# Turning both heads' probabilities with one DMA transposition per query block

## The chip, the cores and the metric

One NeuronCore of one Trainium2 chip runs the whole program. The metric is the device time of one execution in microseconds (us); the figure for the kernel before is the median of three runs. Of one execution there is a profile with a trace: TensorE (PE, with its weight loads as PEld), VectorE (DVE), ScalarE (ACT), GpSimd (POOL), and the sync engine SP, which issues the DMAs.

## The reference

One decoder layer over 16 meta tokens and 512 real positions, model width 1024. From one projection of the normalized input come two attention branches of 16 heads each: MLA (low-rank queries and keys with a rotary part) and FoX (forget gates, added to the scores as differences of a running sum). Both use the same causal attention:

```python
s = jnp.einsum('bhqd,bhkd->bhqk', qb, k, preferred_element_type=jnp.float32) * scale
if cq is not None:
    s = s + (cq[..., :, None] - cum[:, :, None, :])
s = jnp.where(key_pos[None, :] <= qpos[:, None], s, -jnp.inf)
p = jax.nn.softmax(s, axis=-1)
return jnp.einsum('bhqk,bhkd->bhqd', p.astype(v.dtype), v)
```

Each branch's result is gated, multiplied by its own output matrix and by a sigmoid gate; the sum goes through one more matrix, is normalized and added to the input.

## The kernel before

The program has three parts: a prologue (normalization, small projections, the first queries and keys), the attention part (its last `ov` matmul starts at 409.6 us) and the merge with the two branch matrices and the output matrix. Products in full precision are made of three half products: operands are split into a high part (ScalarE) and a low remainder (VectorE or GpSimd), and `passes` and `unit` multiply high by high, low by high and high by low.

The attention part has 16 stages, two heads each: for pair 0 to 7 first the FoX stage, then the MLA stage. I number them 0 to 15, so even stages are FoX and odd ones MLA. In a stage:

- `scores(0)` and `scores(1)` multiply queries and keys of query blocks 0 to 2 and of block 3 (128 queries each, groups `GRP`), VectorE adds the mask and finds the row bound, ScalarE takes the exponential into `sf`.
- `norm(0)` and `norm(1)` divide by the row sums and write the probabilities as 16-bit high and low parts into `pn[0]` (blocks 0 to 2) and `pn[1]` (block 3). ScalarE writes the high parts (L824), VectorE the low ones (L825), GpSimd those of the meta tokens (L811 to L816). Query block b has 2b + 3 tiles of 128 x 128 for each head: one for the meta tokens, and a high and a low one for each key block. That is 3, 5, 7 and 9.
- Then DMA transpositions on SP's queue turn them, one for each block and head, into `pts[0]` and `pts[1]` (keys on partitions, 9 tiles by 512 queries). `pn` and `pts` exist once, and every stage uses them again.
- `values()` multiplies the turned probabilities (`pt`) by the values (`vp`, turned by a DMA transposition as well) into `ov`. It runs after the next stage's `scores(0)`, and its first matmuls read the meta tile of all four query blocks, so it needs the whole set of transpositions.

TensorE's order is the order in which the program is written (`manual_schedule`): between the pieces of a stage stand the projections of the next one (`fq`, `fk`, `mq`, `mk`, `v`, `z`) as filling work. The other engines and SP's queue are ordered by a scheduler, except in a stretch with `keep_in_program_order`. SP takes its instructions one after the other; its queue also holds the weight loads (`wraw`) and the loads of `CT` (forget sums) and `QP` (rotary queries). The DMAs signal through eight semaphores in turn. All issues come from the helper at L91, all matmuls from L97.

`pts` also lends its room, before the first stage, to the rotary queries of the first eight heads (`room`).

Of the kernel before, what the change touches and what calls it, by code (L numbers as in the profile page):

```python
# [11 lines left out]
F32 = mybir.dt.float32  # L12
F32R = mybir.dt.float32r
F16 = mybir.dt.float16
# [9 lines left out]
S = 512  # L24
# [20 lines left out]
PN_STEP = 5  # L45
# [9 lines left out]
def block_kernel(ctx: ExitStack, tc: tile.TileContext, x, meta_tokens, pre_norm_g, w_in, fox_forget_b,  # L55
                 mla_q_norm_g, mla_kv_norm_g, w_uq, w_ukv, w_br_mla, w_br_fox, w_out, post_norm_g,
                 rope_tok, rope_pe, out):
    nc = tc.nc
# [27 lines left out]
    behind, through, first_t, exps, halved, lowered = [], [], [], [], {}, {}  # L86

    def dma(out, src, start=None):

        with tc.issue_after(sums_out[1]) if written[0] and len(sums_out) == 2 else nullcontext():  # L90
            ins = (start or nc.sync.dma_start)(out=out, in_=src)  # L91
        if written[0]:
            tc.keep_in_program_order(ins)
        return ins.ins
# [7 lines left out]
    def split_lo(eng, lo, src, hi):  # L102
        return eng.tensor_tensor(out=lo, in0=src, in1=f32(hi), op=ALU.subtract)  # L103
# [33 lines left out]
    def weights(srcs, wrap):  # L137

        st = {}

        def load():
            if "l" not in st:
                st["l"] = wload(srcs())

        def get():
            load()
            return wrap(wsplit(st["l"]))
        get.load = load
        return get
# [25 lines left out]
    def unit(name, getw, act, nk, sls, done):  # L175

        st = {}
        out = []

        def prep():  # L180
            if "w" not in st:
                st["w"] = getw()
            return True
        for i, sl in enumerate(sls):
            n = sl.stop - sl.start
            for k in range(nk):
                def fn(i=i, sl=sl, k=k, n=n):
                    if "b" not in st:
                        st["b"] = prep()
                        for load in getattr(out[0][1], "nxt", ()):  # L190
                            load()
                    if k == 0:
                        st["ps"] = acc(f"{name}{i}")
                    ps = st["ps"][:, :n]
                    (wh, wl), (ah, al) = st["w"], act(k)
                    for q, (w, a) in enumerate(((wh, ah), (wh, al), (wl, ah))):
                        mm(ps, w(k), a[:, sl], start=(k == 0 and q == 0), stop=(k == nk - 1 and q == 2))
                    if k == nk - 1:
                        done(i, ps)
                out.append((3 * n / 2.4, fn))  # L200
        out[0][1].prep = prep
        if hasattr(getw, "load"):
            out[0][1].load = getw.load
        return out
# [353 lines left out]
    with ExitStack() as att:  # L558

        att.enter_context(tc.manual_schedule(engines={mybir.EngineType.PE}))  # L560
        ac = att.enter_context(tc.tile_pool(name="ac", bufs=1))
# [8 lines left out]
                                channel_multiplier=1, compare_op=ALU.is_ge, fill=NEG)  # L570


        pn = [ac.tile([128, 2, n, 128], F16, tag=f"pn{g}", name=f"pn{g}") for g, n in enumerate((17, 9))]

        pts = [ac.tile([128, 9, 512], F16, tag=f"pt{h}", name=f"pt{h}") for h in range(2)]

        vh = ac.tile([128, 9, 128], F16, tag="vh", name="vh")
        vps = [ac.tile([128, 9, 128], F16, tag=f"vp{s}", name=f"vp{s}") for s in range(2)]
        nc.gpsimd.memset(vh[:, 0], 0.0)
        for b in range(4):  # L580
            nc.gpsimd.memset(pn[b // 3][:, :, PN_STEP * b % 15, :], 0.0)
        gT = []

        wuqh = wuq.rearrange("p k (h e) -> p k h e", e=NOPE + ROPE)
# [36 lines left out]
        def pe_unit(g):  # L621

            def room():
                if g == 0:
                    return [p.rearrange("p a b -> p (a b)")[:, 0 : 8 * S].bitcast(F32).rearrange("p (c s) -> p c s", c=4)
                            for p in pts]
                return gT[0][:, 4:8], gT[1][:, 4:8]

            def results(x):
                if g == 0:  # L630
                    return gT[x][:, 4:6]
                return room()[x][:, 2:4]
            if g == 0:
                nc.sync.dma_start(room()[0][:, 0:2], rope_pe)
            out = []
            w = {}

            def half(xi, ws=None):
                if ws:
                    w[0] = ws  # L640
                return (lambda k: w[0][2 * xi + k][0]), (lambda k: w[0][2 * xi + k][1])

            def srcs():
                if g:

                    tc.keep_in_program_order(nc.sync.dma_start(room()[0][:, 0:2], rope_pe))
                return [wuqh[:, k, 8 * g : 8 * g + 8, NOPE + 16 * x : NOPE + 16 * x + 16]
                        for x in range(2) for k in range(2)]

            for xi in range(2):  # L650
                get = (lambda: half(1)) if xi else weights(srcs, lambda ws: half(0, ws))

                def done(i, ps, xi=xi):
                    r0, tt = room()
                    for cs in range(2):
                        nc.vector.tensor_tensor(out=tt[:, 2 * xi + cs], in0=ps, in1=r0[:, cs], op=ALU.mult)
                out += unit(f"ppe{g}{xi}", get, cq_act, 2, REAL, done)

            def rest(x):

                tt, rr = room()[1], results(x)
                nc.gpsimd.tensor_tensor(out=tt[:, x], in0=tt[:, x], in1=tt[:, 3 - x], op=(ALU.subtract, ALU.add)[x])
                hi, lo = rr[:, 0], rr[:, 1]
                nc.gpsimd.tensor_copy(hi.bitcast(F32R), tt[:, x])
                split_lo(nc.gpsimd, lo.bitcast(F32R), tt[:, x], hi)
                if g:
                    store(x, 0, 8)
                else:

                    for h in range(2):  # L670
                        for i in range(2):
                            r = 64 * h + 32 * i + 16 * x
                            dma(f32(QP[r : r + 16]), rr[16 * h : 16 * h + 16, i])

            def store(x, a, b):
                for i in range(2):
                    dma(qpe_dram[8 * g + a : 8 * g + b, i, x], results(x)[16 * a : 16 * b, i])
            return out, rest, store
# [66 lines left out]
        def attention(br, pr):  # L745
# [55 lines left out]
            def norm(g):  # L801
                def fn():
                    b0, nb_ = GRP[g][0], len(GRP[g])
                    su, ri = (sums[t][:, :, b0 : b0 + nb_] for t in ("su", "ri"))
                    nc.vector.tensor_scalar(out=su, in0=su, scalar1=1.0 / PSCALE, scalar2=None, op0=ALU.mult)
                    nc.vector.reciprocal(ri, su)

                    mt = aw.tile([128, 2, nb_, META], F32, tag=f"mt{g}", name=f"mt{nm_}{g}", bufs=1)
                    src = sfs[g][:, :, 0 : SF_STEP * nb_].rearrange("p h (b c) -> p h b c", b=nb_)[:, :, :, 0:META]
                    dst = pn[g][:, :, 0 : PN_STEP * nb_].rearrange("p h (b t) c -> p h b t c", b=nb_)[:, :, :, 0]  # L810
                    nc.gpsimd.tensor_tensor(out=mt, in0=src, in1=ri.unsqueeze(3).broadcast_to([128, 2, nb_, META]),  # L811
                                            op=ALU.mult)
                    hi, lo, hi2 = (dst[:, :, :, 32 * i : 32 * i + META] for i in range(3))
                    nc.gpsimd.tensor_copy(hi, mt)
                    nc.gpsimd.tensor_tensor(out=lo, in0=mt, in1=hi, op=ALU.subtract)
                    nc.gpsimd.tensor_copy(hi2, mt)  # L816
                    for b in GRP[g]:
                        for h in range(2):
                            sf = sf_of(h, b)[:, META:].rearrange("p (j c) -> p j c", c=128)
                            t0 = PN_STEP * (b % 3) + 1  # L820
                            hi, lo = (pn[g][:, h, t0 : t0 + 2 * b + 2].rearrange("p (j l) c -> p j l c", l=2)[:, :, i]
                                      for i in range(2))
                            rib = sums["ri"][:, h, b : b + 1]
                            nc.scalar.activation(hi, sf, AF.Copy, scale=rib)  # L824
                            nc.vector.scalar_tensor_tensor(out=lo, in0=sf, scalar=rib, in1=hi, op0=ALU.mult,  # L825
                                                           op1=ALU.subtract)
                    for b in GRP[g]:
                        for h in range(2):
                            t0 = PN_STEP * (b % 3)
                            through[:] = [dma(pts[h][:, 0 : 2 * b + 3, 128 * b : 128 * b + 128],  # L830
                                              pn[g][:, h, t0 : t0 + 2 * b + 3].rearrange("p t c -> p (t c)"),
                                              nc.sync.dma_start_transpose)]
                return fn

            def values():
# [37 lines left out]
        g = gate_unit()  # L873
# [3 lines left out]
        for si, (br, pr) in enumerate(stages):  # L877
# [10 lines left out]
            else:  # L888
                g = gate_unit()
# [308 lines left out]
```

## Time and profile before

| what | value |
|---|---|
| runs | 603.93 us median (603.8 to 607.29) |
| profiled execution | 605.73 us, its span 603.9 us |
| granted TensorE clock | 0.998 |
| DMA packets | 219,961, 93.25 MB, mean 154 GB/s |
| of them under 512 bytes | 133,421 |
| share of the 16 DMA engines' span, SP's queue | 66.4% |

Columns of the quoted views: in the waits, the waiting engine with its group, the releaser, then total us, number of waits and the longest. In a timeline, start and length in us, the engine with its line, then the operation with what it writes and reads, and in brackets the idle time ahead of it. A group of SP's issues shows shortest, median and longest in ns. The span is the time from the first to the last instruction of the program.

### The profile page before, as it was taken

The page shows a single profiled execution, that of the slowest core. Times are in us where ns is not written, and L with a number is a line of the kernel's source. Part 1 is how long each engine was busy: PE and PEld are TensorE (multiplying, and loading weights), DVE is VectorE, ACT ScalarE, POOL GpSimd, SP SyncE. Part 2 cuts the span into 40 slices and gives each one's busy share as a digit, 9 for nine tenths or more (in the row PEclk, how much of TensorE's full clock was granted, in tenths as well). Part 3 has the DMA queues.
Part 4 walks back from the last instruction along what each step waited for, and adds up shares of the span by engine and source line. Part 5 has one row for each costly group of instructions (what it writes and reads, how often), then busy time and mean ns, then how long its engine had stood idle before and what let it go on. Part 6 is the DMA issues. An engine that isn't in the chain of part 4 may idle for free.

```text
span 603.9 us, 10999 instructions
## 1 busy us (share of the span) xinstructions
PE 592.4 (98%) x3777; PEld 503.0 (83%) x3777; DVE 374.5 (62%) x1004; ACT 342.9 (57%) x786; POOL 180.1 (30%) x239
## 2 busy tenths in 40 slices
PE   8999999899999999999999999999999999999996
PEld 6889789789889889878898898888888888888884
DVE  5856776674675674765756657773733524367857
ACT  7847774774773784765757748761222433343653
POOL 4316544443348353443433534430000000000000
PEclk9999999999999999999999999999999999999999
DMA  8532689899696898997796985987534323333603
GB/s 286 112 85 87 138 193 201 193 190 228 97 189 147 175 190 164 189 206 164 141 173 165 167 192 135 197 165 267 186 105 104 104 77 99 104 99 91 230 0 140
DMA packets 219961, 93.25 MB, mean 154 GB/s; under 512 B 133421, under 2 KB 211637, under 8 KB 219905
## 3 DMA queue, kind: packets, MB, share of 16 engines
q1 hardware_dynamic: 219904, 92.55, 66.4%
q8 instruction: 30, 0.49, 0.3%
q14 instruction: 27, 0.21, 0.1%
HBM read 58.10 MB, written 4.00 MB: 103 GB/s over the span
## 4 chain that ended last, share of the span: by engine, by line
PE 94%; DMA 2%; ACT 2%; DVE 1%; issue 0%; SPq 0%; POOL 0%; DVEq 0%; ACTq 0%; POOLq 0%
PE z L97 16%; PE pg L97 15%; PE py L97 14%; PE v L97 9%; PE st L97 8%; PE fk L97 8%; PE fq L97 7%; PE ov L97 5%; PE x L97 4%; PE psm L97 3%; PE mq L97 2%; DMA pt<-pn 1%; PE mk L97 1%; PE ppe L97 1%; PE y L97 1%; DMA wsr<-in_w_in_dram 1%
## 5 line engine op out<-in xcount | busy, mean ns | idle before, releaser
L103 POOL TENSOR_TENSOR wl<-wraw,wh 128x1024 fp32r<-128x1024 f32 (+2 forms) x62 | 119.8, 1940 | 107.6 <-ACT wh L130 78.5
L130 ACT CAST wh<-wraw 128x1024 fp32r<-128x1024 f32 (+1 forms) x80 | 83.1, 1042 | 117.3 <-PE pg L97 38.5
L797 ACT ACTIVATE sf<-sf,nb 128x144 f32<-128x144 f32 (+3 forms) x128 | 72.0, 564 | 8.9 <-DVE nb L789 8.7
L825 DVE SCALAR_TENSOR_TENSOR pn<-sf,ri,pn 128x128 f16<-128x128 f32 (+3 forms) x128 | 68.8, 576 | 12.5 <-ACT pn L824 12.5
L824 ACT ACTIVATE pn<-sf,ri 128x128 f16<-128x128 f32 (+3 forms) x128 | 61.5, 551 | 20.1 <-ACT sf L797 17.3
L103 DVE TENSOR_TENSOR wl<-wraw,wh 128x1024 fp32r<-128x1024 f32 x34 | 41.6, 1222 | 42.5 <-ACT wh L130 42.3
L789 DVE CUSTOM_DVE_ANT_0 sf<-st,maskt 128x272 f32<-128x272 f32 (+2 forms) x128 | 48.6, 435 | 3.9 <-PE st L97 3.9
L97 PE MATMUL z<-uTh,wh 128*128 128x512 f32 x128 | 50.9, 398 | 0.0
L97 PE MATMUL pg<-uTh,wh 128*128 128x512 f32 x128 | 50.3, 393 | 0.0
L97 PE MATMUL z<-uTl,wh 128*128 128x512 f32 x128 | 50.1, 391 | 0.0
L97 PE MATMUL z<-uTh,wl 128*128 128x512 f32 x128 | 50.0, 391 | 0.0
L97 PE MATMUL pg<-uTl,wh 128*128 128x512 f32 x128 | 49.8, 389 | 0.0
L97 PE MATMUL pg<-uTh,wl 128*128 128x512 f32 x128 | 49.8, 389 | 0.0
L97 PE MATMUL py<-gh,wh 128*128 128x512 f32 x128 | 49.8, 389 | 0.0
L97 PE MATMUL py<-gl,wh 128*128 128x512 f32 x128 | 49.8, 389 | 0.0
L97 PE MATMUL py<-gh,wl 128*128 128x512 f32 x128 | 49.8, 389 | 0.0
L97 PE MATMUL st<-hlk,hlq 64*128 64x272 f32 (+3 forms) x480 | 47.3, 306 | 0.0
L97 PEld LDWEIGHTS st<-hlk,hlq 64*128 64x128 f32 x480 | 35.0, 185 | 5.8 <-ACT vh L721 2.8
L97 PE MATMUL ov<-pt,vp 128*64 128x256 f16 (+4 forms) x416 | 33.7, 307 | 3.0 <-DMA pt<-pn 2.0
L702 DVE TENSOR_REDUCE vsc<-v 128x1 f32<-128x272 f32 (+1 forms) x32 | 13.1, 432 | 37.9 <-PE v L97 37.9
L97 PE MATMUL v<-uTh,wl 128*128 128x256 f32 (+1 forms) x128 | 36.5, 285 | 0.0
L97 PE MATMUL fk<-uTl,wh 128*128 128x256 f32 (+1 forms) x128 | 36.5, 285 | 0.0
(233 smaller groups left out, 1437.1 us busy)
## 6 DMA issues: line engine op xcount, KB each, us to landing
wraw<-in_w_in_dram SPq DMA_DIRECT2D x56, 512.0 KB
wraw<-in_w_br_fox_dram SPq DMA_DIRECT2D x8, 512.0 KB
tb<-in_w_out_dram SPq DMA_DIRECT2D x8, 512.0 KB
wraw<-in_w_br_mla_dram SPq DMA_DIRECT2D x8, 512.0 KB
wraw<-in_w_out_dram SPq DMA_DIRECT2D x6, 512.0 KB
pt<-pn SPq DMA_TRANSPOSE x128
xr<-in_x_dram SPq DMA_DIRECT2D x4, 512.0 KB
out_dram<-yo SPq DMA_DIRECT2D x8, 256.0 KB
```

Source lines behind the costliest of these rows:

```text
L97: nc.tensor.matmul(*a, **k)
L103: return eng.tensor_tensor(out=lo, in0=src, in1=f32(hi), op=ALU.subtract)
L130: nc.scalar.copy(wh[:, :n], raw[:, :n])
L702: nc.vector.tensor_reduce(out=sc[:, i : i + 1], in_=ps, op=ALU.max, axis=AX.X, apply_absolute_value=True)
L789: nc.vector.tensor_tensor_reduce(out=sf_of(h, b)[:, c0 : c0 + w], in0=ps[h][:, o : o + w], in1=maskt[:, m0 : m0 + w], scale=-scale, scalar ...
L797: exps[g] = nc.scalar.activation(sf, sf, AF.Exp, bias=sums["nb"][:, h, b : b + 1], scale=-1.0, accum_out=sums["su"][:, h, b : b + 1]).ins
L824: nc.scalar.activation(hi, sf, AF.Copy, scale=rib)
L825: nc.vector.scalar_tensor_tensor(out=lo, in0=sf, scalar=rib, in1=hi, op0=ALU.mult, op1=ALU.subtract)
```

## The change

The two heads' tiles of a query block now lie alternately: `pn` is indexed by tile, then head, and one tensor `ptt` of 18 tiles replaces the two of 9, with `pts[h]` as its views of every second tile. One transposition then turns both heads of a block: 6, 10, 14 and 18 tiles, four issues a stage instead of eight. `room`, the clearing of `pn` and the writes of `norm` follow the new indexing. The arithmetic, the bytes moved and the sizes of the tensors stay.

```diff
-        pn = [ac.tile([128, 2, n, 128], F16, tag=f"pn{g}", name=f"pn{g}") for g, n in enumerate((17, 9))]
-        pts = [ac.tile([128, 9, 512], F16, tag=f"pt{h}", name=f"pt{h}") for h in range(2)]
+        pn = [ac.tile([128, n, 2, 128], F16, tag=f"pn{g}", name=f"pn{g}") for g, n in enumerate((17, 9))]
+        ptt = ac.tile([128, 18, 512], F16, tag="pt", name="pt")
+        pts = [ptt.rearrange("p (t h) c -> p h t c", h=2)[:, h] for h in range(2)]
...
-                            hi, lo = (pn[g][:, h, t0 : t0 + 2 * b + 2].rearrange("p (j l) c -> p j l c", l=2)[:, :, i]
+                            hi, lo = (pn[g][:, t0 : t0 + 2 * b + 2, h].rearrange("p (j l) c -> p j l c", l=2)[:, :, i]
                                       for i in range(2))
...
                     for b in GRP[g]:
-                        for h in range(2):
-                            t0 = PN_STEP * (b % 3)
-                            through[:] = [dma(pts[h][:, 0 : 2 * b + 3, 128 * b : 128 * b + 128],
-                                              pn[g][:, h, t0 : t0 + 2 * b + 3].rearrange("p t c -> p (t c)"),
-                                              nc.sync.dma_start_transpose)]
+                        t0, n = PN_STEP * (b % 3), 2 * b + 3
+                        through[:] = [dma(ptt[:, 0 : 2 * n, 128 * b : 128 * b + 128],
+                                          pn[g][:, t0 : t0 + n].rearrange("p t h c -> p (t h c)"),
+                                          nc.sync.dma_start_transpose)]
```

On TensorE, VectorE, ScalarE and GpSimd every instruction stands where it stood; what changes there is only which DMA a wait names. SP's queue changes. At stage 8, before (`pt_726` and `pt_727` are the two heads' turned probabilities, `pn_724` and `pn_725` the two groups of blocks; the sizes are partitions x tiles x 128):

```order
L91 DMA wraw_3397<-in_w_in_dram 128x8x128
L91 DMA_TRANSPOSE pt_726<-pn_724 128x3x128
L91 DMA CT<-c_dram 2x528
L91 DMA_TRANSPOSE pt_727<-pn_724 128x3x128
L91 DMA CT<-c_dram 2x528
L91 DMA_TRANSPOSE pt_726<-pn_724 128x5x128
L91 DMA_TRANSPOSE pt_727<-pn_724 128x5x128
L91 DMA_TRANSPOSE pt_726<-pn_724 128x7x128
L91 DMA_TRANSPOSE pt_727<-pn_724 128x7x128
L91 DMA_TRANSPOSE pt_726<-pn_725 128x9x128
L91 DMA_TRANSPOSE pt_727<-pn_725 128x9x128
L91 DMA wraw_3589<-in_w_in_dram 128x8x128
```

SP's queue at the same place, after (`pt` holds both heads):

```order
L91 DMA wraw_3361<-in_w_in_dram 128x8x128
L91 DMA CT<-c_dram 2x528
L91 DMA_TRANSPOSE pt<-pn_724 128x6x128
L91 DMA CT<-c_dram 2x528
L91 DMA_TRANSPOSE pt<-pn_724 128x10x128
L91 DMA_TRANSPOSE pt<-pn_724 128x14x128
L91 DMA_TRANSPOSE pt<-pn_725 128x18x128
L91 DMA wraw_3552<-in_w_in_dram 128x8x128
```

Eight transpositions became four, and one load of CT moved ahead of the first. At stage 1 SP's queue before, with the weight loads `wraw` and the rotary queries `QP` among the transpositions:

```order
L91 DMA_TRANSPOSE pt_726<-pn_724 128x3x128
L91 DMA_TRANSPOSE pt_727<-pn_724 128x3x128
L91 DMA wraw_1306<-in_w_uq_dram 128x2x192
L91 DMA wraw_1306<-in_w_ukv_dram 128x256
L91 DMA_TRANSPOSE pt_726<-pn_724 128x5x128
L91 DMA QP<-qpe_dram 128x512
L91 DMA_TRANSPOSE pt_727<-pn_724 128x5x128
L91 DMA_TRANSPOSE pt_726<-pn_724 128x7x128
L91 DMA_TRANSPOSE pt_727<-pn_724 128x7x128
L91 DMA wraw_1354<-in_w_in_dram 128x8x128
L91 DMA_TRANSPOSE pt_726<-pn_725 128x9x128
L91 DMA_TRANSPOSE pt_727<-pn_725 128x9x128
```

SP's queue at stage 1, after:

```order
L91 DMA_TRANSPOSE pt<-pn_724 128x6x128
L91 DMA wraw_1298<-in_w_uq_dram 128x2x192
L91 DMA wraw_1298<-in_w_ukv_dram 128x256
L91 DMA QP<-qpe_dram 128x512
L91 DMA_TRANSPOSE pt<-pn_724 128x10x128
L91 DMA_TRANSPOSE pt<-pn_724 128x14x128
L91 DMA wraw_1345<-in_w_in_dram 128x8x128
L91 DMA_TRANSPOSE pt<-pn_725 128x18x128
```

The load of QP moved ahead of all of block 1's tiles; the weight load `wraw_1345` (`wraw_1354` before) still stands ahead of the last block.

More of the change, by code (lines that the diff above doesn't have):

```diff
@@ L580, in block_kernel @@
         for b in range(4):
-            nc.gpsimd.memset(pn[b // 3][:, :, PN_STEP * b % 15, :], 0.0)
+            nc.gpsimd.memset(pn[b // 3][:, PN_STEP * b % 15], 0.0)
         gT = []
@@ L624, in room @@
                 if g == 0:
-                    return [p.rearrange("p a b -> p (a b)")[:, 0 : 8 * S].bitcast(F32).rearrange("p (c s) -> p c s", c=4)
-                            for p in pts]
+                    return [ptt[:, 8 * n : 8 * n + 8].rearrange("p a b -> p (a b)").bitcast(F32).rearrange("p (c s) -> p c s", c=4)
+                            for n in range(2)]
                 return gT[0][:, 4:8], gT[1][:, 4:8]
@@ L809, in fn @@
                     src = sfs[g][:, :, 0 : SF_STEP * nb_].rearrange("p h (b c) -> p h b c", b=nb_)[:, :, :, 0:META]
-                    dst = pn[g][:, :, 0 : PN_STEP * nb_].rearrange("p h (b t) c -> p h b t c", b=nb_)[:, :, :, 0]
+                    dst = pn[g][:, 0 : PN_STEP * nb_].rearrange("p (b t) h c -> p h b t c", b=nb_)[:, :, :, 0]
                     nc.gpsimd.tensor_tensor(out=mt, in0=src, in1=ri.unsqueeze(3).broadcast_to([128, 2, nb_, META]),
```

## The prediction

> **What bounds the kernel now.** I read the page's busy times and its chain first, then the waits of TensorE, then the chain in order of time, then SP's and VectorE's timelines where that chain leaves TensorE, and last the DMA engines in those stretches.
>
> ```profile
> span 603.9 us, 10999 instructions
> PE 592.4 (98%) x3777; PEld 503.0 (83%) x3777; DVE 374.5 (62%) x1004; ACT 342.9 (57%) x786; POOL 180.1 (30%) x239
> PE 94%; DMA 2%; ACT 2%; DVE 1%; issue 0%; SPq 0%; POOL 0%; DVEq 0%; ACTq 0%; POOLq 0%
> ```
>
> TensorE is busy for 98% of the span and carries 94% of the chain. A change that leaves the matmuls and their order as they are can win only what TensorE waits. Its waits, all of them:
>
> ```profile
> PE spun L97 <- DVE ONE L236: 2.1, 1, 2.1
> PE ov L97 <- DMA pt<-pn: 2.0, 2, 1.4
> PE ov L97 <- PE st L97: 0.9, 1, 0.9
> PE pc L100 <- ACT uTh L382: 0.4, 1, 0.4
> PE psm L97 <- POOL wsh L313: 0.3, 1, 0.3
> ```
>
> The first and the last two are in the prologue, which the change does not touch. The second is the product of the turned probabilities with the values (`ov`), waiting for transpositions (`pt<-pn`). The third stands in front of an `ov` too, and the named engine is TensorE itself, long done, so it is a transposition as well. The chain of waits, in order of time, shows the two places (start, length, what):
>
> ```profile
> 103.93 0.40 PE st L97 x5
> 104.33 3.35 DMA pt<-pn
> 107.68 0.04 issue
> 107.72 2.01 PE ov L97 x22
> ...
> 254.75 3.72 DMA pt<-pn
> 258.48 0.09 issue
> 258.57 2.01 PE ov L97 x22
> ```
>
> The first is stage 1 (0.9 + 0.6 us of wait), the second stage 8 (1.4 us). In each the last transposition of the set lands 3.35 or 3.72 us after SP began to issue it, and `ov` starts at once. So all that transpositions cost TensorE today is 2.0 + 0.9 = 2.9 us, 0.5% of the span. Below it I call 1% (6 us) what can be told from no change.
>
> **Why they land late.** SP's timeline at stage 8 (start, length; x6 is six issues in a row, and the last row is the sixth of them by itself), VectorE's two operations on the last query block there, and the two groups of transpositions that SP issues (shortest, median and longest in ns):
>
> ```profile
> 243.56 2.20 SPq L91 DMA_TRANSPOSE pt<-pn  x1
> ...
> 246.28 1.18 SPq L91 DMA_TRANSPOSE pt<-pn  x1
> 247.56 0.38 SPq L91 DMA_DIRECT2D CT<-c_dram  x1
> 248.04 8.04 SPq L91 DMA_TRANSPOSE pt<-pn  x6
> ...
> 254.75 1.32 SPq L91 DMA_TRANSPOSE pt<-pn  x1
> ```
> ```profile
> 246.28 1.41 DVE L825 SCALAR_TENSOR_TENSOR pn<-sf,ri,pn 128x512 f16<-128x512 f32 x2 [0.84 <-ACT pn L824]
> ```
> ```profile
> L91 SPq DMA_TRANSPOSE pt<-pn x128: 1177/1240/2200, 67.9 to 399.5; - x128
> L91 SPq DMA_TRANSPOSE vp<-vh x16: 1312/1784/4450, 61.2 to 384.8; - x16
> ```
>
> The probabilities of the last block are whole at 246.28 + 1.41 = 247.69, yet their second transposition is issued at 254.75: SP spends 8.04/6 = 1.34 us on each, one after the other. Here the queue's issuing is late, not the data. But the DMA engines are not idle meanwhile (columns: stretch, busy time of each engine, clock, share of the 16 DMA engines, GB/s):
>
> ```profile
> 249.00:256.00 7.00, 7.00 (x54) 5.98 (x54) 4.50 (x15) 4.09 (x8) 3.79 (x3) 1.00 0.80 153
> 256.00:258.40 2.40, 1.14 (x11) 0.53 (x7) 2.25 (x13) 2.22 (x10) 2.23 (x2) 1.00 0.97 180
> 98.00:107.60 9.60, 8.19 (x75) 7.56 (x74) 5.25 (x22) 4.18 (x12) 4.52 (x5) 1.00 1.00 216
> ```
>
> At stage 8 they have holes of 7.0 x 0.20 + 2.4 x 0.03 = 1.47 us up to the landing; at stage 1 (98 to 107.6) none. That decides what earlier issuing can win.
>
> **Issues: eight become four.** The 3-tile issue at 246.28 took 1.18 us and the 9-tile one at 254.75 took 1.32, so a tile adds (1.32 - 1.18)/6 = 0.023 us. My estimate for 6, 10, 14 and 18 tiles is 1.25, 1.34, 1.44 and 1.53 us, 5.6 us a set where eight issues at 1.34 take 10.7. SP can be free some 5 us earlier in each of 16 stages, where the probabilities are ready. Bounds: a double issue costs at least a single one (saving 5.4 us) and at most two (saving nothing); I take the slope, since the two rows measure it.
>
> The Trainium skill ("DMA: Bandwidth & Descriptors", section "Why a DMA increments its semaphore by 16 and not by 1", in its table of issue times) gives earlier generations 631 cycles for a small transposition, and for 8,192 tiles 262,144 cycles, 32 a tile, because each tile is pushed by itself. That speaks against the merge: 631 + 15 x 32 = 1,111 cycles for 18 tiles would be 1.18 x 1,111/631 = 2.08 us and a set 6.9, an estimate from that page. The trace's slope, 0.023/1.18 = 2% a tile, is less than half of the page's 32/631 = 5%, though 9 tiles is the largest it has.
>
> **What that moves at stage 8.** Only the holes close: the same packets must still cross. The last landing moves from 254.75 + 3.72 = 258.47 to 258.47 - 1.47 = 257.0. The first issue was held, 2.20 us from 243.56; after it three more and a CT load take 1.34 + 1.44 + 1.53 + 0.4 = 4.7 us and end near 250.5, so SP no longer binds. `ov` was ready at:
>
> ```profile
> 256.77 0.38 PE L97 MATMUL ov<-pt,vp 80*64 80x512 f16 x1
> ```
>
> It waits 0.2 us before its first matmul instead of 1.42 before its second. Its first ran in front of the wait and now runs behind it, so TensorE gains about 1.42 - 0.2 = 1.2 us; bounds 0 (holes stay, as latency) and 1.42.
>
> **At stage 1** the DMA engines are full, and the weight load that stands ahead of the last transpositions stays ahead of them. Nothing is left out of the queue, so the nearest row says 0; the other bound is the whole 0.9 + 0.6 = 1.5. I take 0.4, near the row, since a share averaged over 9.6 us may hide a short hole.
>
> **The other stages** already make it without a wait, some barely. At stage 12:
>
> ```profile
> 328.28 1.18 SPq L91 DMA_TRANSPOSE pt<-pn  x1
> ...
> 337.09 2.74 SPq L91 DMA_TRANSPOSE pt<-pn  x2
> ```
> ```profile
> 342.98 1.22 PE L97 MATMUL ov<-pt,vp 80*64 80x512 f16 x10
> ```
>
> The last issue begins at 337.09 + 1.37 = 338.5 and lands 3.35 to 3.72 later, at 341.8 to 342.2; `ov` starts at 342.98, 1 us after. Landing earlier wins nothing there: 0.
>
> **The wait that is added.** A merged transposition waits for both heads. At stage 8 the first block's two heads end apart:
>
> ```profile
> 241.08 0.42 DVE L825 SCALAR_TENSOR_TENSOR pn<-sf,ri,pn 128x128 f16<-128x128 f32 x1
> ...
> 242.15 0.34 DVE L825 SCALAR_TENSOR_TENSOR pn<-sf,ri,pn 128x128 f16<-128x128 f32 x1
> ```
>
> That is 242.49 against 241.50, 1.0 us, while SP came to it at 243.56: no cost here, at most 1.0 us on the first of a set elsewhere, against some 5 us gained by its end. Behind it on SP stand the loads of CT, QP and the next weights, for which the next stage's scores and projections wait; they all pass four issues fewer. No queue but SP's is moved: ScalarE, VectorE, GpSimd and TensorE keep their order. [...]
>
> **The layout** (tiles alternating by head) changes strides of the writes into `pn` and of the reads from `pt`, not their counts:
>
> ```profile
> L825 DVE SCALAR_TENSOR_TENSOR pn<-sf,ri,pn 128x128 f16<-128x128 f32 (+3 forms) x128 | 68.8, 576 | 12.5 <-ACT pn L824 12.5
> L824 ACT ACTIVATE pn<-sf,ri 128x128 f16<-128x128 f32 (+3 forms) x128 | 61.5, 551 | 20.1 <-ACT sf L797 17.3
> ```
>
> Runs of 128 halves stay whole, so I take 0. Even 10% more is 6.9 us on VectorE and 6.2 on ScalarE, off the chain, 0.4 us a stage, inside stage 12's 1 us margin. As a gain it is bounded by the same 0: nobody on TensorE waits for these writes.
>
> **The sum.** 1.2 + 0.4 = 1.6 us less: the profiled execution goes from 605.73 (span 603.9) to 604.1 (span 602.3). The median of three runs, 603.93, is 1.8 below the profiled one, and goes to 602.3. With the bounds of both places the gain lies between 0 and 2.9: 601.0 to 603.9.
>
> **Rivals.**
>
> *No gain.* Either the transfer alone is the limit (for it: the share of 1.00 at stage 1 and 0.80 at stage 8; against it: 1.47 us of holes), which gives 603.9 with 0.13. Or an issue costs by the tile, so that 18 tiles take 2 x 1.34 = 2.7 us and four issues as long as eight (against it: 1.18 and 1.32 us for 3 and 9 tiles): again 603.9, with 0.07. The skill's push for each tile, above, is of this second kind.
>
> *Slower: large transpositions move at a worse pace.* The present pace from the row of 249 to 256: 153/0.80 = 191 GB/s, 32,768 bytes a tile, 0.171 us. From 3.35 - 9 x 0.171 = 1.8 us for issue and latency, and from first issue to `ov` at stage 12, 342.98 - 328.28 = 14.7 us, a set of 48 tiles may take (14.7 - 1.8)/48 = 0.27 us a tile. From there on it decides. At half the pace (0.342) a set takes 16.4 + 1.8 = 18.2 us, 3.5 us too long; if the eight stages of this branch are all like stage 12, 8 x 3.5 = 28 us, 632. For it: no transposition over 9 tiles stands in the trace. Against: the pace is set by packets, of which there are as many and as large. 0.11.
>
> *Faster by over 1%.* It needs 6 us where TensorE waits 2.9 for all this; only matmuls running faster could give that. 0.03.
>
> **How the numbers follow.** My forecast (a gain of 0.8 to 2.9 us) has 0.66. Forecast and no gain lie within 1%: 0.86; slower 0.11; faster 0.03. The runs of before reach from 603.8 to 607.29, so the median can lie a little above a case. The range from 600.8 to 605.2 covers the two likely cases with that allowance and leaves out the slow one, the fast one and a few bad draws.
>
> **What would show it.** SP should show 64 transpositions of some 1.2 to 1.6 us. Stage 8's `ov` should wait under 0.5 us, stage 1's about 1; TensorE's busy time should stay at 592. If issues of 18 tiles take 2.6 us, the first rival holds. If new `ov` waits appear in stages 2, 4, 6, 10, 12 or 14, the pace fell. A wait of TensorE for weights would mean that loads issued earlier take bandwidth from transpositions, which I have not priced.

## The result and the profile after

| | before | after |
|---|---|---|
| median of 7 runs | 604.95 us (603.68 to 607.29) | 601.31 us (600.76 to 601.94) |
| profiled execution, its span | 605.73, 603.9 us | 601.22, 599.2 us |
| ratio of times | | 0.9936 [0.9915, 0.9958] |

The time fell by 0.6%, 3.6 us between the medians and 4.5 between the two profiled executions. The forecast was 602.3 in a range from 600.8 to 605.2.

Of the page after, the span, the busy times and the chain's shares by engine:

```profile
span 599.2 us, 10724 instructions
PE 590.7 (99%) x3777; PEld 501.3 (84%) x3777; DVE 374.3 (62%) x1004; ACT 342.4 (57%) x786; POOL 179.4 (30%) x239
PE 96%; ACT 2%; DMA 1%; issue 0%; SPq 0%; DVE 0%; POOL 0%; DVEq 0%; ACTq 0%; POOLq 0%
```

All waits of TensorE after (group, releaser, total us, number, longest):

```profile
PE spun L97 <- DVE ONE L236: 2.1, 1, 2.1
PE pc L100 <- ACT uTh L382: 0.3, 1, 0.3
PE psm L97 <- POOL wsh L313: 0.2, 1, 0.2
```

Only the prologue's waits are left; no `ov` waits for a transposition. TensorE's timeline after shows it at the two places where it did, stage 1 and stage 8: all 26 matmuls in a row, with no idle time in brackets.

```profile
105.15 2.04 PE L97 MATMUL ov<-pt,vp 80*64 80x512 f16 x26
...
253.97 2.04 PE L97 MATMUL ov<-pt,vp 80*64 80x512 f16 x26
```

**Where the time went.** From the start of a stage's `ov` to that of a later one TensorE does the same work in every kernel, so these distances tell what was lost between. After, stage 0 to 2 takes 124.70 - 82.53 = 42.17 us and stage 7 to 9 takes 276.59 - 234.43 = 42.16. Before they took 127.19 - 83.13 = 44.06 and 281.13 - 237.15 = 43.98. So 1.89 and 1.82 us were lost at these two places. The rest of the span's 4.7 us is 0.6 ahead of the first stage (83.13 against 82.53), and single tenths in stages 4 and 10. The two places had 0.93 + 0.59 = 1.52 and 1.42 us of listed waits, 0.4 less each. Most of that is in how a row is drawn: before, a first `ov` matmul stood alone ahead of the last wait with a length of 0.38 us, while 26 in a row take 2.04, 0.08 each. A wait behind a lone matmul thus costs some 0.3 us more than its row says.

**What SP did.** Its timeline after, at stage 1 and from stage 7 into stage 8, and the group of its transpositions in the whole program and in stage 8 alone (ns):

```profile
89.42 1.87 SPq L91 DMA_TRANSPOSE pt<-pn  x1
...
98.00 4.01 SPq L91 DMA_TRANSPOSE pt<-pn  x1
...
225.26 1.23 SPq L91 DMA_DIRECT2D qpe_dram<-gT  x2
226.59 0.40 SPq L91 DMA_DIRECT2D wraw<-in_w_in_dram  x1
231.65 0.35 SPq L91 DMA_DIRECT2D QP<-qpe_dram  x1
232.09 0.39 SPq L91 DMA_DIRECT2D wraw<-in_w_in_dram  x1
232.80 1.68 SPq L91 DMA_TRANSPOSE vp<-vh  x1
...
239.85 1.70 SPq L91 DMA_TRANSPOSE pt<-pn  x1
241.59 0.42 SPq L91 DMA_DIRECT2D CT<-c_dram  x1
242.11 6.56 SPq L91 DMA_TRANSPOSE pt<-pn  x3
```
```profile
L91 SPq DMA_TRANSPOSE pt<-pn x64: 1211/1655/4007, 68.3 to 392.5; - x64
L91 SPq DMA_TRANSPOSE pt<-pn x3: 1333/1668/3362, 242.1 to 245.3; - x3
```

The last three of stage 8 are those of 10, 14 and 18 tiles: 1.33, 1.67 and 3.36 us. The set is issued in 1.70 + 1.33 + 1.67 + 3.36 = 8.1 us and ends at 248.7. The semaphore events in the trace show its last landing at 250.5, 3.5 us ahead of `ov`; at stage 1 it is 103.56, 1.6 ahead.

At stage 1 the first two and the last two transpositions of the set stood like this on SP before; the last one was issued at 104.33 and landed at 107.68:

```profile
91.21 2.48 SPq L91 DMA_TRANSPOSE pt<-pn  x2
...
102.24 3.44 SPq L91 DMA_TRANSPOSE pt<-pn  x2
```

Counted from the start of stage 0's `ov` in each kernel (83.13 and 82.53), the set began 1.2 us earlier after the change, its last issue began 5.7 us earlier (15.47 against 21.20), and its end landed 3.5 us earlier (21.03 against 24.55). Some 2.2 us of the earlier issue were given back, because the transposition of 18 tiles took 5.56 us from issue to landing and the one of 9 tiles 3.35.

From stage 7 into stage 8 SP's timeline read before:

```profile
232.84 1.24 SPq L91 DMA_DIRECT2D qpe_dram<-gT  x2
234.19 0.40 SPq L91 DMA_DIRECT2D wraw<-in_w_in_dram  x1
239.57 0.35 SPq L91 DMA_DIRECT2D QP<-qpe_dram  x1
240.02 0.39 SPq L91 DMA_DIRECT2D wraw<-in_w_in_dram  x1
240.50 1.93 SPq L91 DMA_TRANSPOSE vp<-vh  x1
```

The load of `QP` waits at the head of the queue for the two stores `qpe_dram` to land, 4.8 us before and 4.5 after, and what is behind it waits too. These stores stand behind stage 7's set, and left at 225.26 instead of 232.84. The four issues less in that set are 3.2 us of this (8.68 us of SP instead of 11.88). The set had also begun 4.4 us earlier (216.53 against 220.91), behind a values' transposition whose issue took 1.71 us instead of 4.45. The values' transposition of stage 8 left at 232.80 instead of 240.50: 7.7 us earlier, while TensorE itself is only 2.8 us earlier at that `ov` (253.97 against 256.77).

The stretch around stage 1's transpositions, after (stretch, busy time of each engine, clock, share of the DMA engines, GB/s):

```profile
98.00:107.60 9.60, 9.60 (x102) 8.54 (x101) 4.87 (x22) 5.67 (x18) 5.35 (x5) 1.00 1.09 278
```

Before, this stretch had a share of 1.00 at 216 GB/s. The two stretches do not hold the same transfers, though: five transpositions of the set are issued in it before, and one after. The fairer comparison is from the first issue of the set to its last landing, before and then after, since both kernels issue the same loads around the set in that time:

```profile
91.21:107.68 16.47, 14.98 (x126) 14.19 (x125) 10.73 (x33) 8.61 (x21) 7.36 (x10) 1.00 1.04 205
```
```profile
89.42:103.56 14.14, 14.14 (x112) 13.62 (x111) 9.24 (x23) 6.70 (x16) 7.43 (x10) 1.00 1.13 244
```

About the same traffic, 3.4 MB, passed in 14.1 us instead of 16.5, so the share of 1.00 had not been the limit of the DMA engines.

### The profile page after: what moved, and what is told of

It reads as the page before. It is cut to its first block, busy times and chain, and to the rows that moved or that the text cites. A ratio compares the mean times of both kernels' runs of the same rounds, so it can differ in the third digit from the quotient of the medians.

```text
span 599.2 us, 10724 instructions
## 1 busy us (share of the span) xinstructions
PE 590.7 (99%) x3777; PEld 501.3 (84%) x3777; DVE 374.3 (62%) x1004; ACT 342.4 (57%) x786; POOL 179.4 (30%) x239
## 4 chain that ended last, share of the span: by engine, by line
PE 96%; ACT 2%; DMA 1%; issue 0%; SPq 0%; DVE 0%; POOL 0%; DVEq 0%; ACTq 0%; POOLq 0%
PE z L97 17%; PE pg L97 15%; PE py L97 15%; PE st L97 9%; PE v L97 9%; PE fk L97 8%; PE fq L97 8%; PE ov L97 5%; PE x L97 4%; PE psm L97 3%; PE mq L97 2%; PE mk L97 1%; PE ppe L97 1%; PE y L97 1%; DMA wsr<-in_w_in_dram 1%; ACT uTh L382 0%
## 5 line engine op out<-in xcount | busy, mean ns | idle before, releaser
L825 ACT ACTIVATE pn<-sf,ri 128x128 f16<-128x128 f32 (+3 forms) x128 | 61.5, 551 | 19.9 <-ACT sf L798 17.2
L97 PE MATMUL fk<-uTh,wh 128*128 128x256 f32 (+1 forms) x128 | 36.4, 285 | 0.0
```

Of the source, the lines that this page charges most:

```text
L97: nc.tensor.matmul(*a, **k)
```

## The experiments

The theory was that the number of issues on SP's queue makes the difference. Its rivals were that the layout does, that the order on SP does, or that the size of a single transposition does. Every ratio is to runs of the kernel before on the same chip.

**The kernel after again**, as the measure for the next three on their chip.

> The changed kernel itself beside the next three on one chip: 0.994 of the kernel before, about 3.6 us less, TensorE without a wait for transpositions. If it comes out at 1.00 here, the difference on record was between chips and not between kernels.

600.9 us (600.29 to 601.05), ratio 0.9918 [0.9902, 0.9934], no `ov` wait. The gain is there again.

**The new layout with eight issues.** Each block's tiles are cut in two halves:

```diff
-                        through[:] = [dma(ptt[:, 0 : 2 * n, 128 * b : 128 * b + 128],
-                                          pn[g][:, t0 : t0 + n].rearrange("p t h c -> p (t h c)"),
-                                          nc.sync.dma_start_transpose)]
+                        src = pn[g][:, t0 : t0 + n].rearrange("p t h c -> p (t h c)")
+                        parts = (0, n, 2 * n)
+                        for lo, hi in zip(parts, parts[1:]):
+                            through[:] = [dma(ptt[:, lo:hi, 128 * b : 128 * b + 128], src[:, 128 * lo : 128 * hi],
+                                              nc.sync.dma_start_transpose)]
```

> The new layout, but each block turned by two transpositions of 3, 5, 7 or 9 tiles as before, cut by tile range instead of by head. If the number of issues on SP is the cause: SP takes about 10.7 us a set again, the waits of ov at stages 1 and 8 come back (2.9 us in all, within 1), and the time is 604 to 605. If the layout itself is the cause: no such wait and about 601.3.

603.88 us (602.03 to 605.77), ratio 0.9971 [0.9954, 0.9989], 3.0 us above the kernel after on this chip. One wait for transpositions is back in TensorE's list:

```profile
PE ov L97 <- issue: 1.2, 1, 1.2
```

It is at stage 1. The profiler found no releaser, but the first half of the last block, which holds its meta tiles, lands at 105.95, and `ov` starts at 106.04. The second half lands at 107.32, when `ov` already runs: this cut goes by tile range, and `ov` reads the last tiles last. A cut by head, as in the kernel before, would have had to wait for this half too. At stage 8 the last one lands at 254.5, 0.5 us ahead of `ov`. So the layout alone keeps little of the gain. How little is told by the run of the kernel before below.

**Merged in two stages only, and in all but these.** The same code with one of these lines:

```diff
-                        parts = (0, n, 2 * n)
+                        parts = (0, 2 * n) if (br, pr) in stages[0:2] else (0, n, 2 * n)
...
+                        parts = (0, 2 * n) if (br, pr) in stages[2:] else (0, n, 2 * n)
```

> As e1, but merged in stages 0 and 1 only. Issue count: the wait of stage 1 (0.9 + 0.6 us) is gone and that of stage 8 (1.4 us) stays, 1.5 us or 0.25% less than e1. If the transfer is the limit in stage 1, as the share of 1.00 said: stage 1 still waits 1 us or more.

> As e1, but merged in stages 2 to 15 only. Issue count: the wait of stage 1 stays at 1.5 us, that of stage 8 is gone; 1.4 to 2 us less than e1. If the gain at stage 8 needs the earlier stages too (a backlog carried on from stage to stage from the start), stage 8 still waits some of its 1.4 us.

Merged in stages 0 and 1: 601.13 us (600.45 to 601.91), ratio 0.9923 [0.9906, 0.9939], and no `ov` wait in the whole program, not at stage 8 either. Merged in stages 2 to 15: 602.54 us (601.64 to 603.51), ratio 0.9948 [0.993, 0.9965]; TensorE's list has stage 1's wait:

```profile
PE ov L97 <- issue: 1.4, 1, 1.4
```

Eight merged issues do nearly all that 64 do. The place that counts is stage 1. Stage 8 does not wait in the kernel with eight issues in every stage either, so these two runs say nothing of it.

**Sixteen issues a stage.** Each block is cut in four:

```diff
-                        parts = (0, n, 2 * n)
+                        parts = (0, b + 1, n, n + b + 1, 2 * n)
```

> The new layout with each block turned by four transpositions (16 a stage, of 1 to 5 tiles). Issue count: 16 issues at some 1.17 us are 18.7 us of SP in a stage of about 20 us that has other loads to issue (5 us or more), so SP is the bound in the attention part: 4 us or more in each of 16 stages, 660 us or more. If the pace of the packets were the limit and not SP, the time stays at 604 to 606, since bytes and packets are the same.

729.92 us (two runs, 728.11 and 731.73), ratio 1.2028 [1.1978, 1.2079]. The two largest waits of TensorE, and the group of SP's transpositions:

```profile
PE ov L97 <- DMA pt<-pn: 64.9, 46, 11.7
PE ov L97 <- issue: 18.0, 3, 7.6
```
```profile
L91 SPq DMA_TRANSPOSE pt<-pn x256: 1119/1221/3247, 68.0 to 530.2; - x128
```

The bytes are the same. A set now takes 16 x 1.22 = 19.5 us of SP, while the shorter of the two stage lengths above is near 19.5 in all (105.15 to 124.70). SP's timeline over one set, and the stretch of DMA and TensorE around it:

```profile
317.00 5.32 SPq L91 DMA_TRANSPOSE pt<-pn  x4
...
322.90 2.47 SPq L91 DMA_TRANSPOSE pt<-pn  x2
...
325.94 12.96 SPq L91 DMA_TRANSPOSE pt<-pn  x10
```
```profile
311.18:342.90 31.72, 19.43 (x133) 14.53 (x132) 11.91 (x41) 13.65 (x31) 9.30 (x12) 0.78 0.60 129
```

The sixteen issues take 5.32 + 2.47 + 12.96 = 20.75 us, and SP issues with hardly a gap from 311.2 to 342.8, while the DMA engines have a share of 0.60 and TensorE is busy for 19.4 of 31.7 us. So SP binds here, and its issues are a cost by their number.

**Transpositions by themselves.** Behind the last stage the kernel after turns old probabilities again, results unused, in this order of sizes:

```diff
+        probe = pn[1].rearrange("p t h c -> p (t h c)")
+        cols = [(18, 0), (9, 0), (18, 0), (9, 0), (14, 0), (7, 0)]
+        cols += [(6, 0), (10, 1), (14, 2), (18, 3), (18, 3), (14, 2), (10, 1), (6, 0)]
+        for n, c in cols:
+            tc.keep_in_program_order(nc.sync.dma_start_transpose(out=ptt[:, 0:n, 128 * c : 128 * c + 128], in_=probe[:, 0 : 128 * n]))
```

> The changed kernel with 14 more transpositions after the last stage (their results are not used): 18, 9, 18, 9, 14 and 7 tiles into the same place, each after the one before has landed, and then 6, 10, 14, 18 and 18, 14, 10, 6 into four places. If an issue costs 1.11 us and 0.023 us a tile, 18 tiles alone take about 1.5 us, and the 3.2 us of the changed kernel's stages is a hold by a full queue. If an issue costs more for a large one, 18 tiles alone take about 3 us too. Landing of 18 tiles from the start of the issue: 4.9 us at 0.171 us a tile; less if a large one moves faster.

SP's timeline has the first one, of 18 tiles, and the group of all 14:

```profile
404.97 3.49 SPq L973 DMA_TRANSPOSE pt<-pn  x1
```
```profile
L973 SPq DMA_TRANSPOSE pt<-pn x14: 1212/1642/4006, 405.0 to 448.7; - x14
```

| tiles | issue, first six (us) | first issue to landing (us) |
|---|---|---|
| 18 | 3.49 and 2.85 | 5.12 and 6.16 |
| 14 | 1.68 | 4.33 |
| 9 | 1.30 and 1.28 | 3.27 and 3.29 |
| 7 | 1.22 | 3.00 |

From 7 to 9 tiles the slope is small, (1.30 - 1.22)/2 = 0.04 us a tile; between 14 and 18 tiles the issue jumps by 1.2 us or more. This is one run, of 609.87 us with the added work. The first one jumps without another transposition ahead of it, so transpositions ahead on the queue are not needed for it. A weight load had been issued less than 2 us before each of the two, so that the jump comes from such a load is not excluded; the 14 tiles had one as well, and took 1.68.

**The largest block in two.** Only block 3 is cut, into two of 9 tiles, to see whether the slow issue of 18 costs anything:

```diff
-                        parts = (0, 2 * n)
+                        parts = (0, n, 2 * n) if b == 3 else (0, 2 * n)
```

> The changed kernel with the last block cut into two transpositions of 9 tiles, five issues a set. If the long issue of 18 tiles is only a hold, the two halves take about as long together, the last landing is the same within 0.5 us and no wait of ov appears: 1.000 of the changed kernel. If the size itself is dear, the set lands some 0.5 us or more earlier.

601.51 us (600.96 to 601.93), ratio 0.9912 [0.9891, 0.9933]. At stage 12 the halves take 1.64 + 1.42 us of SP and land 15.6 us after the start of stage 11's `ov`; the whole one in the kernel after takes 3.24 and lands 16.1 after it. Neither makes `ov` wait. So merging block 3 is worth nothing by itself, and its slow issue costs nothing.

**Issues without bytes.** Behind each merged transposition SP gets two stores of 64 bytes, their values unused, so that the number of issues is above that of before while the transpositions stay merged:

```diff
+                        for _ in range(2):
+                            with tc.issue_after(through[0]):
+                                nc.sync.dma_start(spare[spared[0]], eps_t[0:1, 0:16])
+                            spared[0] += 1
```

> The changed kernel with two stores of 64 bytes behind each transposition (8 more issues a stage that move nearly no bytes; the stored values are not used). If SP's issuing time is the cause, 8 x 0.4 to 0.5 us = 3 to 4 us of SP a stage gives back most of the 3 to 5 us that the merge saved, and waits of ov come back in part, 1 to 3 us in all: 602 to 604.5. If a large transposition's faster pace or the fewer waits on it were the cause, no wait comes back: 601.3.

606.84 us (604.74 to 608.4), ratio 1.0007 [0.999, 1.0024]: the gain is gone, and more than was expected. TensorE's two new waits, and ScalarE's timeline at the source of the larger one:

```profile
PE mk L100 <- DVE sil L742: 3.3, 1, 3.3
PE ov L100 <- DMA spare<-eps_t: 0.5, 1, 0.5
```
```profile
107.83 1.05 ACT L133 CAST wh<-wraw 128x1024 fp32r<-128x1024 f32 x1 [4.58 <-DMA wraw<-in_w_in_dram]
```

The larger wait is not for a transposition. ScalarE's cast of a weight load waited 4.58 us, the exponentials behind the cast were late, and `mk` waited at the end of that chain. In the kernel after, that cast starts at 103.64. Late issues thus reach TensorE by a second way, the weights. But the scheduler also chose another order with the stores: in the kernel after this load is issued at 96.68, ahead of the transposition of 18 tiles, here at 103.93, behind it. By these times most of what this run lost comes from the order and not from the number of issues. What the stores themselves did is seen on the set: its last issue began 18.38 us after the start of stage 0's `ov`, 2.9 later than in the kernel after, and it landed at 104.96, 0.3 us too late for `ov`. The stores also add 128 landings for the queue to follow, so the time of this run doesn't price an issue.

**The kernel before, measured like a changed one**, and **the eight issues in the order of before** (stage 1's weight load put back behind block 2's transpositions, by a wait in the load of weights):

```diff
-            dma(rv, src)
+            with tc.issue_after(hold.pop()) if hold and w == 1024 else nullcontext():
+                dma(rv, src)
...
+                if si == 1:
+                    hold.extend(through)
```

> The kernel before itself, for a second trace and as a control: ratio 1.000 within 0.002. If the waits of the first trace belong to the kernel, ov waits again at stages 1 and 8, 1 us or more each; if the wait of stage 8 is one execution's chance, it is absent here or elsewhere.

> As e1 (new layout, eight transpositions a stage), with the one weight load of stage 1 put back behind the transpositions of the third block, where the kernel before has it: SP's order is then that of before but for one load of CT. e1 was 1.2 us faster than before. If that came from SP's order in stage 1, this one is at before's time, 605, and waits at stage 1 about 1.5 us. If it came from the layout or from cutting by tile range, it stays at e1's 603.9.

The kernel before: 605.64 us (602.35 to 607.47), ratio 0.9972 [0.9951, 0.9994] to itself. So 0.3% of a ratio here may be no change at all. TensorE's waits for transpositions in this execution:

```profile
PE ov L97 <- issue: 1.9, 1, 1.9
PE ov L97 <- DMA pt<-pn: 0.6, 1, 0.6
```

Both are at stage 1. Stage 8's wait is not in the list: the set landed at 257.45, just as `ov` came (257.20). The order of before with eight issues: 603.27 us (602.07 to 606.39), ratio 0.9954 [0.993, 0.9979], with 1.7 us of wait at stage 1. SP's order explains nothing, then. The two kernels with eight issues in the new layout, 0.9971 and 0.9954, lie at or a little under the 0.9972 of no change. That the layout is worth up to 1 us is not excluded by the times; that it brings the gain is. Their waits at stage 1 are shorter than those of the kernel before because of the cut by tile range, not because the queue is faster: their sets end as late as before (the last table below).

**Stage 7's stores a stage earlier.** In the kernel before, the rotary stores of stage 7 are made in stage 6, so that `QP` and what is behind it no longer wait for them:

```diff
-                if 6 <= si < 8:
+                if si == 6:
...
-                    rest1(si - 6)
+                    rest1(0)
+                    rest1(1)
```

> The kernel before with the rotary stores of stage 7 made in stage 6 already. In the traces SP stood 4.8 us at the load of QP ahead of stage 8, waiting for these stores, with the transpositions of stage 8 behind it. If this is what made stage 8 late, its wait of 1.4 us goes without any merging, and the time falls by 1 to 1.5 us against before; stage 1 waits as before. If eight issues are too many by themselves, stage 8 still waits 1 us or more.

607.34 us (603.56 to 608.94), ratio 1.0008 [0.9982, 1.0034]. The expected gain did not come. `QP` left at 229.16 and stage 8's set landed at 260.1, 0.5 us ahead of `ov`, with no wait there. But the time did not fall, and since the kernel before can be without stage 8's wait too, this doesn't settle what that wait came from. Stage 1, which the edit does not touch, waited longest of all here, and its `ov` then ran slower too (25 matmuls in 3.67 us). The stretches ahead of the wait's end and behind it show why: the granted clock of TensorE was 1.00 up to 109.0 and 0.50 from 110.3 to 113.5 (the column ahead of the DMA share).

```profile
PE ov L97 <- issue: 3.7, 1, 3.7
PE ov L97 <- DMA pt<-pn: 0.6, 1, 0.6
```
```profile
100.00:109.00 9.00, 5.32 (x53) 4.85 (x52) 4.81 (x21) 3.31 (x8) 1.70 (x4) 1.00 1.00 211
110.30:113.50 3.20, 3.20 (x25) 2.37 (x21) 0.36 (x2) 2.69 (x10) 1.95 (x5) 0.50 1.16 323
```

So this wait cost 1.7 us more than its length. After the 1.9 and 0.6 us of the second execution of the kernel before, the clock stayed at 1.00.

**Side by side.** What the profiled executions lost against the kernel after, by the starts of `ov` as above, and when the last transposition of the set landed by the semaphore events, counted from the start of the `ov` one stage earlier. At 22.6 us (stage 1) and 19.5 us (stage 8) `ov` could start. All in us:

| kernel | issues a stage | lost, stage 0 to 2 | stage 1's set lands | lost, stage 7 to 9 | stage 8's set lands |
|---|---|---|---|---|---|
| before | 8 | 1.89 | 24.6 | 1.82 | 21.3 |
| before, second execution | 8 | 2.90 | 25.6 | 0.31 | 19.8 |
| before, stores of stage 7 earlier | 8 | 6.29 | 27.3 | 0.04 | 19.1 |
| new layout | 8 | 1.50 | 25.2 | 0.01 | 19.0 |
| new layout, order of before | 8 | 1.71 | 25.3 | 0.00 | 19.2 |
| merged in stages 2 to 15 | 8, then 4 | 1.73 | 25.4 | 0.00 | 16.1 |
| merged in stages 0 and 1 | 4, then 8 | -0.01 | 21.2 | 0.01 | 18.9 |
| block 3 in two | 5 | 0.00 | 21.9 | -0.02 | 16.3 |
| after | 4 | 0 | 21.0 | 0 | 16.1 |
| after, second execution | 4 | 0.00 | 22.1 | 0.01 | 15.8 |
| after with stores | 4 and 8 stores | 4.31 | 22.9 | 0.02 | 17.5 |

Every kernel with eight issues in stages 0 and 1 loses 1.5 us or more in stage 1, in an amount that changes from one to the next, and its set lands 1.9 to 4.7 us too late, in either layout. None with four or five transpositions and nothing more on the queue loses any; its set lands 0.6 to 1.6 us early. At stage 8 the sets of eight land from 0.6 us early to 1.8 us late, those of four or five 3.2 to 3.7 us early. So stage 8 is on the edge with eight issues: its loss is in one execution of the kernel before, small in another, and nowhere else.

## Why the forecast came out as it did

The mechanism was right: fewer issues on SP, transpositions that land earlier, no other change on TensorE. The forecast gain of 1.6 us was too small, against 3.6 between the medians and 4.5 between the profiled executions; both lie above the bounds of 0 to 2.9 that were given for it.

- **"All that transpositions cost TensorE today is 2.0 + 0.9 = 2.9 us."** As a bound it was too tight. By the distances between `ov` starts it was 1.89 + 1.82 = 3.7 in that execution, since a wait behind the lone first matmul costs some 0.3 beyond its row.
- **Issues.** Forecast 1.25, 1.34, 1.44 and 1.53 us, measured 1.70 (with a hold; the shortest of the group is 1.21), 1.33, 1.67 and 3.36. The slope from 3 to 9 tiles still fitted 10, was short at 14 and failed at 18, twice as far as it was measured. The estimate from the Trainium skill ("DMA: Bandwidth & Descriptors", section "Why a DMA increments its semaphore by 16 and not by 1") was 2.08 for 18 tiles, nearer but short. It set the smallest cycles of its table equal to the 1.18 us of a 3-tile issue, which no run shows to be the same thing, and a cost that grows evenly with the tiles would not leave 10 tiles at 1.33. A set takes 8.1 us where it took 10.7, and the run with block 3 in two shows that the dear issue does no harm.
- **Stage 8: "Only the holes close."** This step failed in size. It placed the landing at 257.0; it was 250.5, and TensorE was only 2.7 us earlier there (234.43 against 237.15 at stage 7's `ov`). The step moved only the set's own issues and left what stands ahead of them. But the stores, `QP` and the values' transposition all left some 7.7 us earlier, and were out of the set's way: before, the set's first transposition landed 5.3 us after its issue, after the change 2.9. TensorE gained 1.8 us there against the 1.2 of the sum, as no more than the wait can be won. And that the wait was there at all was chance: the second execution of the kernel before lost 0.31.
- **Stage 1: "Nothing is left out of the queue, so the nearest row says 0."** This is the term that was most mis-sized, 0.4 where 1.89 was won. A share of 1.00 was read as full DMA engines. The same stretch of the kernel before, 98.0 to 107.6, in 40 slices (a digit is the busy share of 0.24 us in tenths, 9 is 90% or more) has holes, which the average hid:

```profile
DMA  0993999969999739999468889999999999999995
```

  The set and the loads around it then passed in 14.1 us instead of 16.5. The prediction named a hidden hole as possible, and priced it too low.
- **The other stages, the wait that was added, the layout on VectorE and ScalarE**, each put at 0: no `ov` waits, and the writes of the probabilities cost what they did (68.8 and 61.5 us before):

```profile
L826 DVE SCALAR_TENSOR_TENSOR pn<-sf,ri,pn 128x128 f16<-128x128 f32 (+3 forms) x128 | 68.7, 575 | 12.4 <-ACT pn L825 12.3
L825 ACT ACTIVATE pn<-sf,ri 128x128 f16<-128x128 f32 (+3 forms) x128 | 61.5, 551 | 19.9 <-ACT sf L798 17.2
```

- **The rivals.** *No gain* fell with the waits, though its sign was there: an 18-tile issue above 2.6 us. But four issues still end sooner than eight, 8.1 against 10.7 us, and the rest of the queue gains on top of it. *Slower* needed more than 0.27 us a tile; the transpositions by themselves give (5.12 - 3.27)/9 = 0.21 from 9 to 18 tiles, and the stages named for it have no wait. *Faster by over 1%* fell too: there was no more to win than the waits.
- **The base.** The 603.93 of three runs was at the low end of what the kernel before does: 604.95 in seven, 605.1 to 606.2 as the median of 13 to 28 on three other chips. This is why a gain of twice the forecast ends only 1.0 us below the forecast time: the base was 1.0 us too low and the gain 2.0 too small, and the two errors offset each other in part. That the time lies within the range owes something to this luck.

Not settled: whether the layout has up to 1 us of the gain (the sets land no earlier by it), whether an 18-tile issue is slow by itself or is held by something else, and what the size of a transposition does by itself in blocks 0 to 2, since only block 3 was cut alone. No version beats the kernel after, and none can by much on this path: TensorE has only waits of the prologue left.

## What to carry to other kernels

Count what one queue issues in a stage and put it beside the stage's length: here a set of 10.7 us on an in-order queue was late in one stage in every profile and on the edge in another, and doubling the issues cost 20%. When issues are taken off such a queue, follow everything behind them, over stages, and not only the transfers that were merged. To size a wait that may go, take a second profile of the same kernel first, and compare the distances between the same instructions rather than the rows of the waits.

## What was not expected of the hardware

- The spread went with the waits. The profiler's and timed runs of the kernel after have spans from 598.5 to 599.5 us, those of the kernel before from 600.6 to 608.2. Part of it is the clock: every run of the kernel before with a span above 606 us had a mean granted clock of 0.992 to 0.996, every one below 603 of 0.997 to 1.0. A likely reading, not shown for these runs, is that the scatter of late landings becomes the kernel's, and that long waits lower the clock on top of it.
- SP spent 3.36 us (stage 8) and 4.01 (stage 1) on issuing a transposition of 18 tiles, and 1.67 on one of 14. With nothing but a weight load ahead, 18 tiles still took 3.49.
- A DMA share of 1.00 left room: with the same loads around it, stage 1's set had a share of 1.04 at 205 GB/s before and of 1.13 at 244 after.
- With sixteen issues a stage, TensorE was granted a clock of 0.929, against 0.999 after, and the same 3,777 matmuls kept it busy for 630.3 us instead of 590.7. The execution with a wait of 3.7 and 0.6 us in a row shows it in small: behind it the clock was 0.50 from 110.3 to 113.5. A wait of TensorE can cost more than its length.
